# A new order from re-measured planner prices, one seven-product pair fewer, and a handicap for late GpSimd steps

## The chip, the cores and the metric

The kernel runs on one core of a Trainium2 chip. The metric is the device time of one execution in microseconds (us). TensorE (PE, its weight loads PEld) multiplies into PSUM, VectorE (DVE), ScalarE (ACT) and GpSimd (POOL) do the rest, and SyncE (SP) issues most DMA transfers. Each engine works through its own queue in order; steps on different engines are tied by semaphores.

## The reference

One pre-norm layer on x of 512 tokens x 1024 channels in float32, with two token mixers fed by one input projection:

```python
h = rmsnorm(x, norm_g)
(q_lat, c_kv, k_rope, z_a, q_b, k_b, v_b, z_b,
 q_idx, k_idx, w_idx, gate_a, gate_b) = jnp.split(h @ w_in, cuts, axis=-1)
# branch a: 8-head latent attention (low-rank q and kv, rotary key), causal in chunks of 64
y_a = mla_attention(q_nope, q_pe, k_nope, k_pe, v_a, pos) * silu(z_a)
# branch b: an indexer scores keys, each query keeps its top 128; relative bias; 8 heads
y_b = dsa_attention(q_b, k_b, v_b, q_idx, k_idx, w_idx, rel_bias, pos, topk) * silu(z_b)
merged = sigmoid(gate_a) * (y_a @ w_o_a) + sigmoid(gate_b) * (y_b @ w_o_b)
out = rmsnorm(x + merged @ w_out, final_g)
```

## The kernel before

**Products.** A number in float32 is split into a rounded high part and a rest (a cast on ScalarE, L370, and a subtraction on VectorE or GpSimd, L401 or L403), and each product is three matmuls (high x high, high x rest, rest x high; `mm3`, all recorded at L479). The input is held transposed and normalised as eight k-tiles `hT`. A projection tile of 128 output channels comes in one of two ways. `proj` (L1139), the plain one, multiplies eight k-tiles by all 512 tokens: 24 matmuls of 512 columns. `proj2` (L1203) takes two tiles as a 2 x 2 block product and needs seven products instead of eight (Strassen's scheme in Winograd's form): sums of weights and of inputs (`input_sums`, L1170, tiles `hs`) come first, each product is four k-tiles by 256 tokens, and `seven` (L1289) takes partial sums out of PSUM into the tiles `pair`.

**Stages.** The first 50 us load x and the first weights and make latents and indexer keys. Then come the projections of the a branch (gates `ga`, `za`, the MLA operands `ma`, values `va`) while the indexer's scores and the top-128 masks are made (`topk`, L964), with a's attention heads in between; then pairs of b's projections (`SB` keys and queries, `VB` values, `GB` gates, `ZB` the SiLU gates z_b) with b's heads in between. `branch_out` (L2076) multiplies each branch by its w_o, `merged` (L2050) splits the result, and `output` (L2279) multiplies by w_out, again by seven products numbered 1, 7, 2, 6, 5, 4, 3, whose weights are summed and split in `out_job` and `split_b` (L2134, L2125, tiles `wsum` and `wo`). `finish` and `scale_out` (L2187, L2227) add x, normalise and store. Gates of branch a are stored to HBM after their tanh (`gate`, L1462, transfer bias_scratch<-s_sig) and fetched back late.

**What sets the order.** The program is written as threads that yield steps; while it is built, a planner (`Flow`, L154, its loop `run` at L214) keeps a clock for each engine, prices every ready step, and emits the one that can start first. Steps with two possible engines (`BOTH`, VectorE or GpSimd) go where they would end first, with a handicap for GpSimd (`pbias`; `soon`, L393, sets it to 0, and `LATE` sets the general one once the last mask is made, L978). Prices stand in the step helpers: ScalarE in `act_opt` (L365), VectorE and GpSimd in `tt`, `ts` and `scale_by` (L397, L418, L426), TensorE in `stream` and `turn` (the transposes, L470 and L492). The delay of a semaphore is in `lat` (L156). A transfer's bytes over 360000 are its duration, times `SLOWER`, then `LAND` (L255 to L257). The chip's queues follow the order so planned; the prices themselves appear nowhere in the program that runs. `QUEUE` (L2446) is the list of projection and output jobs, with pairs in capitals. Further constants limit the slots a class may hold (`PHCAP`, `TCAP`, `PCAP`, `SPARE`) and set the priorities of threads.

## Time and profile before

| | |
|---|---|
| median of 3 runs | 425.13 us (423.97 to 425.34) |
| the profiled execution's own time | 425.56 us |
| its span, first to last instruction | 423.8 us, at a granted clock of 0.996 |
| ScalarE busy | 297.5 us (70%) |
| GpSimd busy | 100.9 us (24%) |
| DMA | 65.91 MB, mean 156 GB/s |

The span is the time between the first and the last instruction; the execution's own time is 1.8 us longer. A busy share is an average over all stages, and TensorE's busy time counts a matmul until its results are out, although the next one has begun by then. So the rows by stage and the waits say more than the shares.

### The profile page before, as it was taken

What the parts mean: (1) busy time and instruction counts of PE and PEld (TensorE: products, weight loads), DVE (VectorE), ACT (ScalarE), POOL (GpSimd) and SP (SyncE); (2) the same over time, 40 slices, a digit from 0 to 9 for tenths busy, and PEclk for the clock granted to TensorE, in tenths of its full rate; (3) what the DMA queues carried; (4) which work ended last, traced back from release to release, by engine and by line L of the source; (5) the groups of instructions that cost most, each with busy time, mean ns of one, the idle gap of its engine ahead of it and who ended that gap; (6) DMA issues with size and microseconds to landing.
All of it is one profiled execution on the core that took longest, in us unless ns stands there. A gap on an engine that the chain in (4) does not pass through costs nothing.

```text
span 423.8 us, 7541 instructions
## 1 busy us (share of the span) xinstructions
PE 413.6 (98%) x2487; PEld 368.8 (87%) x2487; DVE 378.7 (89%) x804; ACT 297.5 (70%) x682; POOL 100.9 (24%) x127
## 2 busy tenths in 40 slices
PE   9999999999999999999999999999999999999983
PEld 6999888898887888889999999999998888888863
DVE  4879789899999999997999789899869997999994
ACT  5796976479584967749786798997689744347534
POOL 1033764024344547541000012130001000010212
PEclk9999999999999999999999999999999999999998
DMA  8973345724644631442334737314633975566305
GB/s 266 394 285 101 116 137 183 182 57 110 202 104 152 179 111 49 125 113 76 113 130 105 200 95 199 95 65 136 187 113 125 336 254 200 182 201 209 134 1 199
DMA packets 30279, 65.91 MB, mean 156 GB/s; under 512 B 4648, under 2 KB 5688, under 8 KB 30240
## 3 DMA queue, kind: packets, MB, share of 16 engines
q1 hardware_dynamic: 29120, 63.82, 48.1%
q0 software_dynamic: 832, 1.22, 1.1%
q8 instruction: 19, 0.31, 0.3%
q10 hardware_dynamic: 288, 0.39, 0.3%
q14 instruction: 20, 0.16, 0.1%
HBM read 50.49 MB, written 4.21 MB: 129 GB/s over the span
## 4 chain that ended last, share of the span: by engine, by line
PE 65%; DVE 20%; ACT 5%; issue 4%; DMA 2%; POOL 1%; SPq 1%; POOLq 0%; DVEq 0%; ACTq 0%
PE ps L479 57%; PE ps L498 4%; DVE s_wo L401 2%; DVE s_mg L401 2%; ACT s_w L370 2%; DVE s_w L401 1%; DVE s_wsum L401 1%; DMA raw<-w_out 1%; DVE s_rg L401 1%; DVE s_x L413 1%; DVE mask L972 1%; DVE s_pair L401 1%; PE ps L606 1%; PE ps L946 1%; DVE s_xr L413 1%
## 5 line engine op out<-in xcount | busy, mean ns | idle before, releaser
L479 PE MATMUL ps<-s_h,s_w 128*128 128x512 f32 (+1 forms) x672 | 139.2, 350 | 0.0
L479 PEld LDWEIGHTS ps<-s_h,s_w 128*128 128x128 f32 x672 | 106.6, 189 | 13.4 <-ACT s_w L370 0.2
L370 ACT CAST s_w<-raw 128x512 fp32r<-128x512 f32 (+3 forms) x134 | 77.4, 596 | 18.5 <-DVE raw L401 9.3
L401 DVE TENSOR_TENSOR s_w<-raw,s_w 128x512 fp32r<-128x512 f32 (+2 forms) x104 | 67.1, 663 | 6.9 <-ACT s_w L370 6.2
L479 PE MATMUL ps<-s_hs,s_w 128*128 128x256 f32 x384 | 53.5, 285 | 0.0
L403 POOL TENSOR_TENSOR s_w<-raw,s_w 128x512 fp32r<-128x512 f32 (+2 forms) x30 | 35.0, 1173 | 77.6 <-DVE s_ys L413 36.9
L479 PEld LDWEIGHTS ps<-s_hs,s_w 128*128 128x128 f32 x384 | 49.2, 191 | 0.4
L479 PE MATMUL ps<-s_ys,s_w 128*128 128x512 f32 x192 | 43.7, 389 | 0.0
L479 PEld LDWEIGHTS ps<-s_ys,s_w 128*128 128x128 f32 x192 | 36.0, 188 | 7.6
L479 PE MATMUL ps<-s_wo,s_mg 128*128 128x512 f32 (+1 forms) x156 | 33.6, 374 | 1.2 <-ACT s_wo L370 0.9
L479 PEld LDWEIGHTS ps<-s_wo,s_mg 128*128 128x128 f32 x156 | 27.6, 188 | 7.0 <-ACT s_wo L370 1.3
L479 PE MATMUL ps<-s_w,s_xg 128*128 128x328 f32 (+1 forms) x192 | 32.9, 324 | 0.1
L479 PEld LDWEIGHTS ps<-s_w,s_xg 128*128 128x128 f32 x192 | 31.3, 188 | 0.6 <-ACT s_rbc L370 0.5
L379 ACT ACTIVATE s_p<-s_p,sm 128x512 f32<-128x512 f32 (+3 forms) x58 | 31.6, 564 | 0.1
L972 DVE MATCH_REPLACE8 mask<-sm,mask 128x256 f32<-128x256 f32 (+2 forms) x48 | 25.8, 540 | 0.0
L971 DVE MAX8 sm<-mask 128x8 f32<-128x256 f32 (+2 forms) x48 | 25.5, 547 | 0.3
L498 PE MATMUL ps<-ident,s_p 128*128 128x128 f32 x160 | 23.0, 274 | 0.0
L379 ACT ACTIVATE s_p<-ps,sm 128x128 f32<-128x128 f32 (+3 forms) x32 | 16.7, 525 | 8.9 <-DVE sm L1878 8.8
L370 ACT COPY s_tmp<-ps 64x512 f32<-64x512 f32 (+1 forms) x18 | 10.1, 562 | 15.5 <-PE ps L479 8.7
L498 PEld LDWEIGHTS ps<-ident,s_p 128*128 128x128 f32 x160 | 18.4, 140 | 2.6 <-DVE s_ph L401 0.5
L479 PE MATMUL ps<-s_lat,s_w 128*128 128x512 f32 x78 | 20.5, 394 | 0.0
L1977 DVE CUSTOM_DVE_ANT_0 s_p<-ps,mask 128x128 f32<-128x128 f32 (+3 forms) x32 | 15.3, 486 | 4.9 <-PE ps L479 4.7
(217 smaller groups left out, 798.4 us busy)
## 6 DMA issues: line engine op xcount, KB each, us to landing
raw<-w_out SPq DMA_DIRECT2D x18, 512.0 KB, 5.2
s_op<-s_op SPq DMA_DIRECT2D x36, 128.0 KB, 2.4
raw<-w_ga SPq DMA_DIRECT2D x8, 512.0 KB, 3.4
raw<-w_gb SPq DMA_DIRECT2D x8, 512.0 KB
raw<-w_o SPq DMA_DIRECT2D x16, 256.0 KB, 4.5
s_x<-xT SPq DMA_DIRECT2D x8, 256.0 KB, 4.0
s_xn<-x SPq DMA_DIRECT2D x8, 256.0 KB, 5.6
raw<-w_za SPq DMA_DIRECT2D x4, 512.0 KB, 5.0
```

Source lines behind the costliest of these rows:

```text
L370: nc.scalar.copy(dst.ap, src.ap)
L379: nc.scalar.activation(dst.ap, src.ap, func, **kw)
L401: opts.append(("DVE", 0.07 + 0.00104 * x.n, lambda: nc.vector.tensor_tensor(dst.ap, x.ap, y.ap, op=op)))
L403: opts.append(("POOL", 0.15 + 0.0021 * x.n, lambda: nc.gpsimd.tensor_tensor(dst.ap, x.ap, y.ap, op=op)))
L413: lambda: nc.vector.scalar_tensor_tensor(dst.ap, x.ap, sc(s), y.ap, op0=op0, op1=op1))],
L479: nc.tensor.matmul(ps.ap, l.ap, r.ap, start=start and i == 0, stop=stop and i == len(pairs) - 1, skip_group_check=more)
L498: nc.tensor.transpose(d.ap, s.ap, ident.tile)
L606: nc.tensor.matmul(ps.tile.rearrange("p (a b) -> p a b", b=P), z, z.rearrange("p (a b) -> p a b", a=1).to_broadcast([P, NT, P]), start=Tru ...
L946: yield pe(0.005 + n / 2400, [ps.all], [qs[h].all, ks[0].all], lambda: (product_to(ps[:, :n], True), nc.tensor.matmul(ps.tile[:, :n], qs[h ...
L971: yield Step([("DVE", t, lambda: nc.vector.max(m8.tile, work.ap))], [m8], [mask[i]])
L972: yield Step([("DVE", t + 0.068, lambda: nc.vector.match_replace(work.ap, m8.tile, work.ap, MARK))], [mask[i]], [m8])
L1977: step = Step([("DVE", 0.1 + 0.00104 * n, lambda: nc.vector.tensor_tensor_reduce(p.ap, ps.tile[:, :n], mask[i].tile, op0=ALU.add, op1=ALU. ...
```

## The change

Three things change, all of them in how the order is planned. First, the planner's prices: the delay before TensorE goes from 0.26 to 0.19 us, ScalarE's and VectorE's delays become a little shorter; steps on fewer than 128 partitions get 0.12 us more, some activations 0.075 to 0.1 more; a transpose goes from 0.109 to 0.0875, a 512-column matmul from 0.228 to 0.227; transfers after the first 25 us have three kinds (inside SBUF, loads, stores) with prices of their own. Second, the queue of jobs: ZB0 and ZB3 become plain tiles (zb0 right behind sb0, zb3 behind the last gate pair), and ZB1 and ZB2 form one pair. Third, the weight sums and rests of the output products other than 1, 7 and 2 carry a handicap of 0.4 us on GpSimd, and the general handicap after the last mask goes from 0.75 to 0.4. Limits of slots and priorities are set anew.

```diff
@@ Flow.lat
         if dst == "PE":
-            return 0.26
-        return {"PE": 0.2, "ACT": 0.15, "DVE": 0.16, "POOL": 0.08}[src]
+            return TO_PE
+        return {"PE": 0.2, "ACT": 0.14, "DVE": 0.12 if dst == "ACT" else 0.16, "POOL": 0.08}[src]
@@ Flow.run, a transfer of SP
-                self.hw = max(self.hw, s) + (0.65 if step.ins and step.outs else 0.475)
-                self.dma = max(self.dma, self.hw + 0.65) + dur * (SLOWER[bool(step.ins and step.outs)] if s > 25.0 else 1.0)
-                end = self.dma + (LAND if step.ins and step.outs else 1.5 if s < 0.77 or dur < 0.05 else 2.15 if s < 10.0 else 1.8 if s < 20.0 else 1.0) + step.late
+                kind = 0 if step.ins and step.outs else 1 if step.outs else 2
+                if s > 25.0:
+                    at = max(self.hw, s)
+                    self.hw = at + 0.59
+                    self.dma = max(self.dma, at + 1.0) + dur * SLOWER[kind]
+                    end = self.dma + LAND[kind] + step.late
...
@@ step helpers
+    def few(x):
+        return 0.12 if x.ap.shape[0] < P else 0
...
+    def late(step, product):
+        step.pbias = 0.0 if product in EARLY else LATE
+        return step
...
-        return max(0.0148 + n / 2400, 0.109) - 0.0015 * (n == 256)
+        return max(0.0134 + n / 2400, 0.109)
...
-        return pe(0.109 * len(parts), [d for d, _ in parts], [s for _, s in parts] + [ident.all], emit, len(parts))
+        return pe(0.0875 * len(parts), [d for d, _ in parts], [s for _, s in parts] + [ident.all], emit, len(parts))
...
-            yield Step([("DVE", t + 0.068, lambda: nc.vector.match_replace(work.ap, m8.tile, work.ap, MARK))], [mask[i]], [m8])
+            yield Step([("DVE", t - 0.009, lambda: nc.vector.match_replace(work.ap, m8.tile, work.ap, MARK))], [mask[i]], [m8])
@@ split_b and out_job
-        yield soon(lo_part(lo.all, raw, hi.all))
+        yield late(lo_part(lo.all, raw, hi.all), key[0])
...
-                    yield soon(tt(t, raw[i], t, ALU.add if product == 6 else ALU.subtract, BOTH))
+                    yield late(tt(t, raw[i], t, ALU.add if product == 6 else ALU.subtract, BOTH), product)
@@ constants
-PHCAP = 6
+PHCAP = 5
-TCAP = 6
-PTOPK = 15.0
-PSCORE = 12.0
+TCAP = 5
+PTOPK = 13.0
+PSCORE = 10.0
-QUEUE = 'ga0 ga1 pe ma0 ga2 za0 va1 va0 ma1 ga3 za1 ma2 ga4 ga5 ma3 za2 za3 sb0 ga6 ga7 VB SB1 GB0 GB1 SB2 ZB0 ZB1 GB2 GB3 SB3 GB4 GB5 ZB2 ZB3 gb6 ou ou gb7 ou'
-LATE = 0.75
+QUEUE = 'ga0 ga1 pe ma0 ga2 za0 va1 va0 ma1 ga3 za1 ma2 ga4 ga5 ma3 za2 za3 sb0 zb0 ga6 ga7 VB SB1 GB0 GB1 SB2 ZB1 ZB2 GB2 GB3 SB3 GB4 GB5 zb3 gb6 ou ou gb7 ou'
+LATE = 0.4
+EARLY = (1, 7, 2)
-YSB = 7
+YSB = 5
-LAND = 2.6
-SLOWER = 1.08, 2.0
+LAND = 1.5, 1.3, 1.4
+SLOWER = 1.8, 1.13, 1.09
+TO_PE = 0.19
-PLOW = 8.0
-PREST = 3.0
-SPARE = {'w': 2, 'wo': 6, 'sig': 3}
+PLOW = 9.0
+PREST = 8.0
+SPARE = {'w': 3, 'wo': 6, 'sig': 3}
-PSUMS = 5.0
-PCAP = 10
+PSUMS = 8.0
+PCAP = 11
-SUMS_AT = ('a', 5)
+SUMS_AT = ('a', 6)
```

More of the change, by code (lines that the diff above doesn't have):

```diff
@@ L254, in run @@
                 self.free["SP"] = s + 0.05
-                self.hw = max(self.hw, s) + (0.65 if step.ins and step.outs else 0.475)
-                self.dma = max(self.dma, self.hw + 0.65) + dur * (SLOWER[bool(step.ins and step.outs)] if s > 25.0 else 1.0)
-                end = self.dma + (LAND if step.ins and step.outs else 1.5 if s < 0.77 or dur < 0.05 else 2.15 if s < 10.0 else 1.8 if s < 20.0 else 1.0) + step.late
+                kind = 0 if step.ins and step.outs else 1 if step.outs else 2
[4 more added lines that the diff above has]
+                    end = self.dma + LAND[kind] + step.late
+                else:
+                    self.hw = max(self.hw, s) + (0.475 if kind else 0.65)
+                    self.dma = max(self.dma, self.hw + 0.65) + dur
+                    end = self.dma + (1.5 if s < 0.77 or dur < 0.05 else 2.15 if s < 10.0 else 1.8 if s < 20.0 else 1.0) + step.late
             else:
@@ L287 @@
 JITTER = 0
-SEED = 687
+SEED = 1
 DRAWN = random.Random(SEED)
@@ L363, in bufs @@
         return [v.buf for v in vs if isinstance(v, View)]
+    def few(x):
+        return 0.12 if x.ap.shape[0] < P else 0
     def act_opt(dst, src, func=AF.Copy, scale=None, bias=None, accum=None):
         t = (0.05 if in_ps(src) else 0.1) + 0.00083 * src.n + ((0.18 if in_ps(src) else 0.09) if accum is not None else 0) + (0.09 if isinstance(scale, View) else 0)
+        t += (0.1 if isinstance(bias, View) and not in_ps(src) else 0) + few(src) + (0.075 if func == AF.Square else 0)
         def emit():
@@ L400, in tt @@
             if e == "DVE":
-                opts.append(("DVE", 0.07 + 0.00104 * x.n, lambda: nc.vector.tensor_tensor(dst.ap, x.ap, y.ap, op=op)))
+                opts.append(("DVE", 0.07 + 0.00104 * x.n + few(x), lambda: nc.vector.tensor_tensor(dst.ap, x.ap, y.ap, op=op)))
             else:
@@ L418, in ts @@
     def ts(dst, x, s1, s2, op0, op1=None):
-        t = 0.1 + (0.00104 if in_ps(x) else 0.00052) * x.n
+        t = 0.1 + (0.00104 if in_ps(x) else 0.00052) * x.n + few(x) + 0.03 * isinstance(s1, View)
         kw = {} if op1 is None else {"op1": op1}
@@ L430, in scale_by @@
             if e == "DVE":
-                t = 0.1 + (0.00104 if in_ps(x) else 0.00052) * x.n
+                t = 0.13 + (0.00104 if in_ps(x) else 0.00052) * x.n
                 opts.append((e, t, lambda: nc.vector.tensor_scalar(dst.ap, x.ap, s.ap, None, ALU.mult)))
```

## The prediction, before the result was known

> **What bounds the kernel now.** I read the page first: the busy shares, then the slices.
>
> ```profile
> span 423.8 us, 7541 instructions
> PE 413.6 (98%) x2487; PEld 368.8 (87%) x2487; DVE 378.7 (89%) x804; ACT 297.5 (70%) x682; POOL 100.9 (24%) x127
> PEclk9999999999999999999999999999999999999998
> ```
>
> TensorE is busy 98% of the span at the full granted clock, and VectorE comes next with 89%. A time can therefore go down in three ways only: fewer or cheaper TensorE instructions, fewer waits of TensorE, or a shorter tail behind its last matmul. The 98% is not proof of no waits, because a matmul's busy time overlaps the next one's, so I read the busy time by stage next, and then who made TensorE wait. In the rows by stage the columns are the stretch, its length, and busy microseconds (instructions) of PE, PEld, DVE, ACT and POOL, then clock, DMA share and GB/s.
>
> ```profile
> 120.00:140.00 20.00, 19.38 (x106) 16.34 (x105) 19.03 (x51) 11.90 (x30) 9.13 (x12) 1.00 0.46 137
> 340.00:360.00 20.00, 20.00 (x90) 16.57 (x89) 16.12 (x28) 8.85 (x15) 0.00 (x0) 1.00 0.62 218
> 360.00:380.00 20.00, 20.00 (x90) 16.48 (x89) 19.97 (x38) 7.68 (x14) 1.93 (x3) 1.00 0.60 190
> 380.00:400.00 20.00, 20.00 (x93) 16.69 (x92) 19.29 (x37) 14.30 (x29) 1.59 (x2) 1.00 0.58 197
> 400.00:424.00 24.00, 15.89 (x88) 13.14 (x86) 18.47 (x39) 9.52 (x23) 4.82 (x6) 0.93 0.23 88
> ```
>
> From 340 to 400 us TensorE never stops, while VectorE is full (19.97 and 19.29 of 20). Only in the last 24 us does TensorE lose real time. The waits of TensorE, longest first, from the views of the weight loads and of the matmuls:
>
> ```profile
> PEld ps L479 <- ACT s_wo L370: 1.3, 1, 1.3
> PEld ps L1894 <- ACT s_p L379: 1.1, 1, 1.1
> PEld ps L498 <- DVE s_lat L413: 1.0, 1, 1.0
> PEld ps L479 <- DVE s_wo L401: 0.6, 1, 0.6
> PEld ps L479 <- ACT ps L370: 0.6, 3, 0.2
> PEld ps L498 <- DVE s_ph L401: 0.5, 2, 0.3
> PE ps L1894 <- ACT s_p L379: 0.6, 1, 0.6
> ```
>
> Apart from the start, these six groups are nearly the whole prize: 5.1 us of idling weight loads, of which the matmuls feel a part. No engine is to be relieved for its own sake.
>
> **Part one: one pair of ZB tiles becomes two plain tiles.** A pair by seven products is 7 x 4 k-tiles x 3 matmuls = 84 matmuls of 256 columns. Two plain tiles are 2 x 8 x 3 = 48 of 512 columns. Both rates stand in the timeline (start, us, count), in the first pair stage and the plain branch stage; two groups of the page follow, with busy time and mean ns of one:
>
> ```profile
> 209.90 3.04 PE L479 MATMUL ps<-s_w,s_h 128*128 128x256 f32 x24
> 212.78 3.04 PE L479 MATMUL ps<-s_w,s_hs 128*128 128x256 f32 x24
> 333.15 13.08 PE L479 MATMUL ps<-s_ys,s_w 128*128 128x512 f32 x57
> ```
>
> ```profile
> L479 PE MATMUL ps<-s_ys,s_w 128*128 128x512 f32 x192 | 43.7, 389 | 0.0
> L498 PE MATMUL ps<-ident,s_p 128*128 128x128 f32 x160 | 23.0, 274 | 0.0
> ```
>
> From 209.90 to 212.78 are 2.88 us for 24, so 0.120 us each. The 57 plain ones take 13.08 us with the last one's own duration (the 389 ns of the page's group) in it, so 12.69 / 56 = 0.227 each. The pair costs 84 x 0.120 = 10.08 us, the two tiles 48 x 0.227 = 10.90 us. **TensorE gets 0.82 us more work.** In a stage where it never rests this lands on the end in full.
>
> The Trainium skill ("TensorE: Matmul & The Clock Gate", section "Wait — 56ns, not 53.3ns?") gives a warm matmul its columns at 2.4 GHz plus about 2.5 ns; by that an estimate is 48 x 0.2158 - 84 x 0.1092 = 1.19 us more. The trace does not agree with the figure (0.227 and 0.120 measured), so the measured 0.82 stands.
>
> What the pair no longer asks of the other engines, from the groups kept apart by shape:
>
> ```profile
> L370 ACT CAST s_w<-raw 128x512 fp32r<-128x512 f32 x110 | 66.6, 621 | 17.6 <-DVE raw L401 9.3 <-DMA raw<-w_o 5.5 <-PE ps L479 2.0
> L401 DVE TENSOR_TENSOR s_w<-raw,s_w 128x512 fp32r<-128x512 f32 x89 | 59.7, 685 | 6.0 <-ACT s_w L370 5.3
> L370 ACT COPY s_pair<-ps 128x256 f32<-128x256 f32 x32 | 11.8, 369 | 7.8 <-PE ps L479 7.5
> L401 DVE TENSOR_TENSOR s_pair<-ps,s_pair 128x256 f32<-128x256 f32 x16 | 6.7, 419 | 1.1 <-PE ps L479 0.8 <-ACT s_pair L370 0.3
> ```
>
> Seven splits become four, four sums of weights go, and five copies and two adds out of PSUM go. On ScalarE that is 3 x 0.62 + 5 x 0.37 = 3.7 us, on VectorE and GpSimd together (3 + 4) x 0.69 + 2 x 0.42 = 5.7 us. None of it is on TensorE's path by itself. It can help only by removing the small waits (ACT ps 0.6, DVE s_ph 0.5) of the attention heads that share this stage. I bound that between 0 and -1.1 and take -0.5, near the middle, since the rows name those engines but each wait is under 0.3. The input sums are also free one pair earlier, and the gated branch can be split sooner; nothing in TensorE's rows waits for these, so 0.
>
> **Part two: the planner's prices.** They emit no instruction; they change which step comes next on each engine. Only their fit to the trace can be judged before:
>
> ```profile
> s_op<-s_op SPq DMA_DIRECT2D x36, 128.0 KB, 2.4
> bias_scratch<-s_sig SPq DMA_DIRECT2D x8, 256.0 KB, 3.8
> 151.38 0.79 PE ps L498 x7
> L370 ACT COPY s_tmp<-ps 64x512 f32<-64x512 f32 x16 | 9.3, 582 | 14.9 <-PE ps L479 8.7 <-DMA bias_scratch<-s_sig 5.9
> L370 ACT COPY s_pair<-ps 128x512 f32<-128x512 f32 x4 | 2.3, 582 | 0.0
> ```
>
> A 128 KB move inside SBUF was priced 0.65 + 0.65 + 0.364 x 2.0 + 2.6 = 4.63 us and becomes 1.0 + 0.364 x 1.8 + 1.5 = 3.16; it lands in 2.4. A 256 KB store was 0.475 + 0.65 + 0.728 x 1.08 + 1.0 = 2.91 and becomes 1.0 + 0.728 x 1.09 + 1.4 = 3.19; it lands in 3.8. Both come closer. Two prices move away: a transpose goes from 0.109 to 0.0875 where seven take 0.79 (0.113 each), and a step on fewer than 128 partitions gets 0.12 more on its engine, where 64 and 128 partitions both take 582 ns. So the plan is better on transfers and not better all over.
>
> The transfers matter at one place. At 135 us ScalarE has waited long for the slot of a stored gate, and TensorE pays soon after:
>
> ```profile
> 135.21 0.58 ACT L370 COPY s_tmp<-ps 64x512 f32<-64x512 f32 x1 [5.87 <-DMA bias_scratch<-s_sig]
> 137.85 0.45 PE L1894 MATMUL ps<-s_op,qhi 100*128 100x384 f32 x1 [0.62 <-ACT s_p L379]
> ```
>
> The idle 0.62 and the 0.16 us by which a 512-column matmul outlasts the next one's start (0.389 less 0.227) make 0.8 us. With a longer price for the store and a shorter one for the moves, this copy should no longer sit first in ScalarE's queue: **-0.8 us** (bounds 0 and -1.8; the second takes in the wait for s_lat, 1.0 at the weight load, which I leave standing). The moved zb0 (ahead of ga6), the tighter limits on slots and the new priorities have no row of their own; I give them 0, with the bounds of the sum of all these waits on one side and of the second and third rival on the other.
>
> **Part three: fewer late GpSimd steps.** In the output stage the sums and rests of products 6, 5, 4 and 3 get a handicap of 0.4 us on GpSimd where they had none; other steps that two engines can do have theirs lowered from 0.75 to 0.4 once the last mask is made, so GpSimd may take more in the attention stages, at no price for TensorE while VectorE is not ahead of it. What it did there, and what came behind the last one:
>
> ```profile
> 393.68 1.30 POOL L403 TENSOR_TENSOR s_wo<-s_wsum,s_wo 128x512 fp32r<-128x512 f32 x1 [13.39 <-ACT s_wo L370]
> 400.08 1.30 POOL L403 TENSOR_TENSOR s_wo<-s_wsum,s_wo 128x512 fp32r<-128x512 f32 x1 [5.10 <-DVE s_wo L401]
> 401.05 1.48 DVE L401 TENSOR_TENSOR s_part<-s_part,s_part 128x512 f32<-128x512 f32 x2
> 396.65 1.28 DVE L401 TENSOR_TENSOR s_wsum<-raw,s_wsum 128x512 f32<-128x512 f32 x2
> 406.22 1.29 POOL L403 TENSOR_TENSOR s_wsum<-raw,s_wsum 128x512 f32<-128x512 f32 x1 [4.84 <-DVE s_xr L401]
> 408.55 0.60 ACT L370 CAST s_wo<-s_wsum 128x512 fp32r<-128x512 f32 x1
> 405.67 2.65 PE L479 MATMUL ps<-s_wo,s_mg 128*128 128x512 f32 x11
> 409.20 0.51 PE L479 MATMUL ps<-s_wo,s_mg 128*128 128x512 f32 x1 [0.88 <-ACT s_wo L370]
> 409.99 1.43 PE L479 MATMUL ps<-s_wo,s_mg 128*128 128x512 f32 x5 [0.28 <-DVE s_wo L401]
> ```
>
> GpSimd makes a sum of weights until 407.51, its cast on ScalarE ends at 409.15, and TensorE resumes at 409.20. The run before ended at 408.32 with a matmul whose next could have started 0.16 us earlier, so 409.20 - 408.16 = 1.04 us are lost; the next start, 409.99, is 0.79 after instead of 0.23, so 0.56 more. **1.6 us**, the largest single loss. On VectorE the sum (half of 1.28 for two, 0.64) would be done by 406.9 from the same start. I take -1.6, with bounds 0 and -1.6. The price of moving three steps is 3 x 0.64 = 1.9 us on a full VectorE if TensorE's stock of operands runs out, and 0 while it holds, as it did from 340 to 408. I take 0. The moved steps issue no DMA and pass no queue of SP.
>
> The two VectorE sums at 401.05 took 1.48 beside a GpSimd step, against 1.28 alone: 0.20 us lost per such meeting, so three moved steps also give VectorE back up to 0.6. The Trainium skill ("SBUF — State Buffer", section "SBUF: two separate sides") has the port pair that the two share as an exclusive lock for a whole instruction; the trace agrees in direction, with 0.20 of a 1.30 us step.
>
> **Sum.** +0.82 - 0.5 - 0.8 - 1.6 + 0 = -2.1 us. The profiled execution took 425.56 us (span 423.8 and 1.76 around it), 0.43 above the median 425.13 of the runs; 425.56 - 2.1 = 423.5 there, 425.13 - 2.1 = **423.0** for the median. The tail behind the last matmul stays as it is.
>
> **The rivals.**
> *The waits only move.* TensorE's order is new in all stages, and VectorE, full from 360 to 400, leaves its last operands as late as before. For it: the 1.6 us came after 40 us of a full VectorE, and its total in that stage hardly falls. Against it: GpSimd and ScalarE, not VectorE, made the last sum late. Then +0.82 stays, only the -0.8 counts, and the time is about 425.1, no difference. A measurement of this kernel can tell about 0.3%, 1.3 us.
> *The late steps overfill VectorE, and it is slower.* If TensorE's stock runs out before 400, each step that GpSimd would have taken costs TensorE 0.64 us: 425.13 + 0.82 + 1.9, with the old 1.6 still there, is 427.9. It decides from the point where VectorE has no idle time ahead of the last rests, and 19.97 of 20 is near. Against it: the pair's 5.7 us of steps are gone from the stage ahead.
> *The plan with too cheap transposes is no better.* The heads' 160 transposes are now planned 0.0215 us shorter, 3.4 us in all, so plan and chip part by more; data is then early rather than late at TensorE, but buffers come free late. If two waits as large as the one at 137.85 return in the attention stages: 425.13 + 0.82 + 2 x 0.8 - 1.6 = 426.0, within what can be told from no change.
>
> **How the numbers follow.** The forecast has 0.57; waits that move and the plan that is no better together 0.25; the overfull VectorE 0.18. The likeliest case reaches from all bounds down (425.13 + 0.82 - 1.1 - 1.8 - 1.6 = 421.4, and 0.6 less with VectorE's gain, 420.9) up to 423.8. Both unchanged cases lie between 425 and 426.1. Of the slower case the lower half, to 426.6, is inside. So 420.9 to 426.6. Faster 0.57, same 0.25, slower 0.18.
>
> **What would show it.** In the changed profile: 28 copies s_pair<-ps of 256 columns instead of 32 (four a pair, so seven pairs), 2451 TensorE instructions; the line "ACT s_wo" gone from TensorE's waits, and no 512-column GpSimd step after about 390; the store of a gate no longer ahead of a 5.87 us wait of ScalarE. I am wrong if TensorE's waits sum to as much as before at other places, or if it stops for VectorE's s_wo rests between 380 and 410.

## The result and the profile after

The changed kernel takes 427.75 us in the median of five executions (426.87 to 429.5), the kernel before 425.13 (423.97 to 425.59). The ratio is 1.0073, 95% interval [1.0056, 1.0091]: slower by about 2.6 us. The forecast was 423.0 in a range from 420.9 to 426.6, so the time went the other way and lies outside the range. The profiled execution of the changed kernel is the slowest of its five, 429.5 us with a span of 427.7. That matters below.

The page of the changed kernel, its first lines and the slices of the granted clock:

```profile
span 427.7 us, 7455 instructions
PE 415.5 (97%) x2451; PEld 369.4 (86%) x2451; DVE 375.5 (88%) x801; ACT 293.5 (69%) x669; POOL 101.6 (24%) x126
PEclk9999999989999999999999999999999999999998
```

TensorE has the 36 matmuls less that the pair's end was to bring, VectorE and ScalarE have 3.2 and 4.0 us less to do, and there is one slice more with a lower clock, the ninth, which begins near 85 us. By stage, with the columns as in the prediction; the first line is the kernel before, the others the changed one:

```profile
80.00:100.00 20.00, 20.00 (x127) 18.10 (x126) 19.59 (x53) 13.33 (x34) 3.46 (x8) 1.00 0.37 107
80.00:100.00 20.00, 18.16 (x107) 16.57 (x106) 16.06 (x47) 11.10 (x31) 3.52 (x6) 0.91 0.15 46
120.00:140.00 20.00, 20.00 (x110) 17.16 (x109) 19.67 (x47) 13.55 (x34) 9.24 (x13) 1.00 0.55 158
240.00:260.00 20.00, 19.35 (x154) 18.77 (x154) 15.43 (x42) 15.92 (x44) 0.00 (x0) 1.00 0.51 151
300.00:320.00 20.00, 19.48 (x138) 17.86 (x138) 17.86 (x34) 15.20 (x37) 0.00 (x0) 1.00 0.74 228
400.00:424.00 24.00, 20.38 (x113) 17.55 (x111) 22.18 (x45) 11.97 (x28) 4.83 (x6) 0.99 0.17 61
```

The stage from 120 to 140 us is better than before (20.00 against 19.38), the one from 80 to 100 is worse (18.16 against 20.00, and 20 matmuls fewer in it). The waits of TensorE's weight loads in the changed kernel name the new ones:

```profile
PEld ps L1910 <- DMA s_op<-kpel: 2.0, 1, 2.0
PEld ps L494 <- ACT s_pair L381: 1.5, 3, 0.8
PEld ps L494 <- ACT s_w L381: 1.0, 2, 0.6
PEld ps L1909 <- ACT s_p L390: 0.8, 2, 0.5
PEld ps L513 <- POOL rstd L468: 0.6, 1, 0.6
```

The waits that the prediction meant to remove are out of this list: the one for s_wo near 409 us, and the one for s_p at 137.85 (the 0.8 for s_p lies at other places). The small ones of the heads that it named (ACT ps, DVE s_ph) are gone too. Others stand instead. From the starts of all matmuls in the two traces I took what each interval has above the pace of its shape (0.227 us for 512 columns, 0.120 for 256). The stream without that excess is 400.1 us before and 400.9 after; the excess is 15.7 before and 18.2 after. So the last matmul starts 3.3 us later (416.77 and 420.10), and the tail behind it is 0.6 us longer (7.0 and 7.6 to the end of the span): the 3.9 us between the spans. By stage the excess grew by 3.4 us from 80 to 100 us, by 1.5 from 240 to 320 and by 1.0 in the first 40; it shrank by 0.8 from 40 to 60, by 0.9 from 120 to 140 and by 1.7 behind 400.

**The wait at 85 us.** TensorE of the changed kernel, then the queue of SP, each with start and duration, then how long the move took from issue to landing:

```profile
79.48 2.91 PE L494 MATMUL ps<-s_h,s_w 128*128 128x512 f32 x12
82.23 0.87 PE L494 MATMUL ps<-s_w,s_lat 128*128 128x256 f32 x6
82.94 0.22 PE L1909 MATMUL ps<-s_op,qhi 100*128 100x128 f32 x1
85.00 0.33 PE L1910 MATMUL ps<-s_op,qhi 96*128 96x128 f32 x1 [1.84 <-DMA s_op<-kpel]
```

```profile
76.93 0.85 SPq L523 DMA_DIRECT2D s_op<-kpeh  x1
77.89 0.40 SPq L523 DMA_DIRECT2D raw<-w_ga  x1
78.35 0.42 SPq L523 DMA_DIRECT2D bias_scratch<-s_sig  x1
78.82 0.58 SPq L523 DMA_DIRECT2D s_op<-kpel  x1
```

```profile
s_op<-kpel SPq DMA_DIRECT2D x2, 64.0 KB, 6.1
```

The first logits of an a head start at 82.94, and their second matmul needs the 64 KB move of kpel. The move is issued behind a 512 KB load of w_ga and a 256 KB store of a gate on the same queue and lands 6.1 us after its issue. The kernel before issues the move behind the same load and store, but 27 value matmuls go first on TensorE from 82.36 us on, so that its logits come at 85.58 and find the data there:

```profile
82.36 3.38 PE L479 MATMUL ps<-s_w,s_lat 128*128 128x256 f32 x27
85.58 0.22 PE L1894 MATMUL ps<-s_op,qhi 100*128 100x128 f32 x1
```
The planner's price of such a move by itself fell from 0.65 + 0.65 + 0.182 x 2.0 + 2.6 = 4.26 to 1.0 + 0.182 x 1.8 + 1.5 = 2.83 us, both far under 6.1, and the plan now puts the logits ahead. Every order below that the planner made with the new price of the moves has this wait in some size, and none made with the old price has it.

**The end.** GpSimd of the changed kernel behind 396 us, and its TensorE:

```profile
398.67 1.29 POOL L418 TENSOR_TENSOR s_wsum<-raw,s_wsum 128x512 f32<-128x512 f32 x1 [25.85 <-DVE s_wsum L416]
403.65 1.30 POOL L418 TENSOR_TENSOR s_wo<-s_wsum,s_wo 128x512 fp32r<-128x512 f32 x1 [3.69 <-DVE s_wsum L416]
414.79 1.31 POOL L418 TENSOR_TENSOR s_wo<-raw,s_wo 128x512 fp32r<-128x512 f32 x1 [9.84 <-DVE s_wo L416]
```

```profile
397.83 16.92 PE L494 MATMUL ps<-s_wo,s_mg 128*128 128x512 f32 x85
414.58 5.80 PE L494 MATMUL ps<-s_wo,qhi 128*128 128x512 f32 x36
```

There are still three GpSimd steps of 512 columns behind 390 us, as many as before, but TensorE runs through to its last matmul. The 1.6 us of waits are gone, and the time is not shorter.

### The profile page after: what moved, and what is told of

The parts are those of the page before. It is cut to its first block, busy times and chain, and to the rows that moved or that the text cites. A ratio compares the mean times of both kernels' runs of the same rounds, so it can differ in the third digit from the quotient of the medians.

```text
span 427.7 us, 7455 instructions
## 1 busy us (share of the span) xinstructions
PE 415.5 (97%) x2451; PEld 369.4 (86%) x2451; DVE 375.5 (88%) x801; ACT 293.5 (69%) x669; POOL 101.6 (24%) x126
## 4 chain that ended last, share of the span: by engine, by line
PE 63%; DVE 17%; DMA 9%; ACT 5%; issue 3%; SPq 2%; POOL 0%; POOLq 0%; ACTq 0%; DVEq 0%
PE ps L494 54%; PE ps L513 5%; DVE s_w L416 2%; DVE s_wo L416 2%; DMA raw<-w_o 2%; DVE s_mg L416 2%; ACT s_w L381 2%; SPq L523 2%; DMA s_op<-kpel 1%; DMA raw<-w_ql 1%; DMA s_x<-xT 1%; DMA s_xn<-x 1%; DVE s_pair L416 1%; DVE s_rg L416 1%; PE ps L1910 1%
## 5 line engine op out<-in xcount | busy, mean ns | idle before, releaser
L494 PE MATMUL ps<-s_h,s_w 128*128 128x512 f32 (+1 forms) x684 | 149.5, 357 | 1.1 <-ACT s_pair L381 0.6
L494 PEld LDWEIGHTS ps<-s_h,s_w 128*128 128x128 f32 x684 | 110.3, 189 | 15.6 <-ACT s_pair L381 1.5
L381 ACT CAST s_w<-raw 128x512 fp32r<-128x512 f32 (+3 forms) x132 | 76.0, 595 | 22.0 <-DMA raw<-w_o 12.7
L416 DVE TENSOR_TENSOR s_w<-raw,s_w 128x512 fp32r<-128x512 f32 (+2 forms) x95 | 62.1, 674 | 3.9 <-ACT s_w L381 3.5
L418 POOL TENSOR_TENSOR s_w<-raw,s_w 128x512 fp32r<-128x512 f32 (+2 forms) x37 | 44.5, 1207 | 61.7 <-ACT s_w L381 30.7
L494 PE MATMUL ps<-s_hs,s_w 128*128 128x256 f32 x336 | 46.7, 285 | 0.0
L494 PEld LDWEIGHTS ps<-s_hs,s_w 128*128 128x128 f32 x336 | 42.8, 191 | 0.4 <-DVE s_w L416 0.2
L390 ACT ACTIVATE s_p<-s_p,sm 128x512 f32<-128x512 f32 (+3 forms) x52 | 28.7, 571 | 0.1
L494 PE MATMUL ps<-s_lat,s_w 128*128 128x512 f32 x78 | 20.7, 397 | 0.0
```

The costliest lines, as they stand in the source:

```text
L381: nc.scalar.copy(dst.ap, src.ap)
L390: nc.scalar.activation(dst.ap, src.ap, func, **kw)
L416: opts.append(("DVE", 0.07 + 0.00104 * x.n + few(x), lambda: nc.vector.tensor_tensor(dst.ap, x.ap, y.ap, op=op)))
L418: opts.append(("POOL", 0.15 + 0.0021 * x.n, lambda: nc.gpsimd.tensor_tensor(dst.ap, x.ap, y.ap, op=op)))
L494: nc.tensor.matmul(ps.ap, l.ap, r.ap, start=start and i == 0, stop=stop and i == len(pairs) - 1, skip_group_check=more)
```

## The experiments

The times of each group of runs stand beside the kernel before on the same chip; ratios are to that. "Replayed" means that the planner follows a recorded list of (thread, engine), so that only the entries named differ in the program; "planned anew" means that the planner chose again, and that every stage may differ.

### What the wait at 85 us costs

Replayed order of the changed kernel, with three moves put forward (the first kpeh is ahead of the load already):

```diff
 SP queue near 77 us
 s_op<-kpeh
+s_op<-kpel, s_op<-kpeh, s_op<-kpel
 raw<-w_ga
 bias_scratch<-s_sig
-s_op<-kpel, s_op<-kpeh, s_op<-kpel
```

> The changed kernel in its own order, with four steps of SyncE's queue moved and nothing else: the four key moves (s_op<-kpeh, s_op<-kpel) are issued ahead of the 512 KB load of w_ga and the 256 KB store of a gate that they followed. Theory A (TensorE's 2.0 us wait at 85 us comes from moves that land in order behind that load and store): the moves land by about 81 us, the wait and the stretch at half clock behind it go, and the median falls by the 2.0 us of the wait, 427.75 to about 425.8, or by up to 3.6 where an execution also had the half clock. Rival B (the changed order loses in many small places, and a wait that is removed returns at the next full buffer or late operand): under 0.7 us of it arrives at the end, 427.1 to 427.8.

426.63 us (425.67 to 427.05) against 424.65, ratio 1.0046 [1.0033, 1.0059]. TensorE in this run, where the second matmul follows the first at once:

```profile
83.11 0.22 PE L2106 MATMUL ps<-s_op,qhi 100*128 100x128 f32 x1
83.18 0.28 PE L2107 MATMUL ps<-s_op,qhi 96*128 96x128 f32 x1
```

Set beside the profiled execution of the changed kernel, TensorE is 3.2 us ahead at 91 us and still 3.2 us ahead at its last matmul: nothing of it is given back. In the medians it is much less, from 1.0073 to 1.0046, with intervals that overlap a little. So the profiled execution overstates the wait: its mean granted clock is 0.991, that of the four other executions 0.993 to 0.994, and the run without the handicap (below) shows a shorter wait at the same place.

Of the 3.2 us the wait itself is 1.9. The rest is in the clock: behind the wait the granted clock was 0.5 from 85.6 to 89.0 us. To keep it up without touching the wait, nine matmuls of zeros went into the bank that the head is about to use; their product is overwritten and read by nothing.

```diff
+for _ in range(9): matmul(bank, zero, zero)   # ahead of the first head's logits
```

> The changed kernel in its own order, with nine matmuls on zeros (0.216 us each) into the PSUM bank of the first attention head, just ahead of its logits, so that TensorE computes instead of waiting at 83 to 85 us; the moves land as late as before. Theory A with the clock (the wait costs twice, because the granted clock falls to one half for 3.4 us behind it in the profile): the wait stays 2 us long but the clock stays full, the profiled execution falls by about 1.7 us (429.5 to 427.8); the median falls by 1.7 too if all executions had the half clock, by little if only the profiled one had. Rival (the half clock is only shown and costs nothing, or comes from something else): the median stays at 427.75 within 0.4.

428.98 us (428.49 to 429.4), 1.0106 [1.0092, 1.0119]. The clock stayed at 1.0 there, and TensorE gained 1.6 us on the changed kernel's profile between 85 and 92 us. But the median rose. The nine matmuls themselves hold TensorE from 83.89 to 85.66 us, also in an execution where the move would have been only a little late; and in the profiled execution the weight load behind GpSimd's power for rstd waited 1.9 us at the start instead of 0.6. Which of the two raised the median is not shown. The clock's part is seen in the profile; as a price in the median this run is inconclusive.

Old prices of the moves alone, planned anew:

```diff
-LAND = 1.5, 1.3, 1.4
-SLOWER = 1.8, 1.13, 1.09
+LAND = 2.9, 1.3, 1.4
+SLOWER = 2.0, 1.13, 1.09
```

> The changed kernel with the planner's price of moves inside SBUF as long as before (LAND 2.9 and SLOWER 2.0 for them), all else as changed; the order from 70 us on is planned anew. Theory A (the shorter price is what put the first logits ahead of their keys): the 2.0 us wait at 85 is gone from TensorE's waits, median about 425.8. Rival B (any new plan loses as much in other places): no wait at 85, but others, and a median between 426.5 and 430.

430.35 us (429.43 to 431.43), 1.0147 [1.013, 1.0164]. The wait at 85 us is gone, as it should be, and the time is worse. Its list begins with a wait that in the changed kernel is 0.6 in all:

```profile
PEld ps L494 <- DVE s_w L416: 3.0, 3, 2.4
```

### Parts of the change, planned anew

The new prices and limits with the old list of two ZB pairs, the first part of the change alone, and the change without it:

```diff
 e4  QUEUE of before, all else changed
 e8  before, with lat(), the transfer prices and the step prices of the change
 e10 the change, with the price table of before
```

> The changed kernel with the queue of jobs of before (ZB0 ZB1 and ZB2 ZB3 as two pairs), all else as changed: the order is the same up to about 170 us, so the wait at 85 us stays. Theory C (the plain ZB tiles cost what they add to TensorE, 0.8 us, and little else): the median falls by 0.8 to about 426.9. Rival (the queue is the main cause, by what the plain tiles displace at 240 to 320 us): it falls by 2 or more, to 425.7 or below. Rival B (a new plan loses elsewhere): it rises above 427.75.

432.12 us (431.58 to 434.9), 1.0196 [1.0169, 1.0223]; the wait for kpel is there with 2.0 us, and many others behind 195 us.

> The first part of the change alone: all prices of the changed kernel, with the queue of jobs, limits, priorities and handicaps of before. Theory A (the better transfer prices are sound but for the moves): the wait at 85 us costs 2 us, the rest gains as much, 1.000 to 1.004. Rival B (queue, limits and prices were chosen together, and any order planned with one of them replaced loses 3 us or more to waits all over, as the two re-planned kernels did with 1.0147 and 1.0196): 1.007 or more, with waits at several places between 190 and 320 us.

430.97 us (428.53 to 432.66), 1.0142 [1.0115, 1.017]; kpel 2.8 us in two waits, s_pair 3.4 in four.

> The change without its first part: the new list of pairs, the handicap for late GpSimd steps and the new limits and priorities, but the price table of before; planned anew. Theory A (the scatter of orders, not a price, decides; the table was only right together with the rest): slower than the changed kernel, 428 to 434 us, with no wait of TensorE behind a kpeh or kpel move near 85 us, but others. Rival B (the new price of the moves is the whole loss, and what the other parts bring is intact): 423 to 425.5 us, no wait over 1 us between 40 and 400 us.

429.87 us (429.65 to 430.12), 1.0113 [1.01, 1.0127]. No wait for kpel, but 2.9 us in four for s_pair. The rival, that the move's price was the whole loss, has nothing for it here; what rules it out is the run with the moves forward, which has no such wait and still stands at 1.0046 [1.0033, 1.0059].

Each of these variants is worse than the whole change. Before reading that as the parts needing one another, the plain question is what a new plan costs that changes nothing. The planner adds a small constant times a thread's priority (20 at most) to each candidate's start. A change of the constant by 0.001 shifts one candidate against another by less than 0.03 us, so it decides near ties alone; the constant stands for nothing on the chip.

```diff
-BIAS = 0.01
+BIAS = 0.011   # e9 on before, e16 on the changed kernel; e15 on before with 0.009
```

> The kernel before with a single planner constant changed that stands for nothing on the chip: the weight of a thread's number in the comparison of candidates, 0.010 to 0.011. It computes the same, with the same instructions on TensorE, but 623 of the 1,106 TensorE steps of the plan stand elsewhere. Theory A (each re-planning gives an order whose small waits are drawn anew, and the order of before is a lucky one of many): slower than before by 0.5 to 2%, 427 to 433 us, with two to five new TensorE waits of 0.5 to 2.5 us that before does not have. Rival B (the plan's order is worth the same unless prices or products change; the losses of the variants came from their parts): within 0.3% of before, 424 to 426.5 us.

426.31 us (425.18 to 426.67), 1.0026 [1.0014, 1.0038].

> The kernel before with the weight of a thread's number in the planner's comparison at 0.009 instead of 0.010: a second neutral order, with 744 of 1,106 TensorE steps elsewhere. Theory A (scatter: an order drawn anew is worth a few tenths to 2% less than the chosen one): 426 to 432 us. Rival B (neutral orders agree within 0.3% and the parts tried alone lost for reasons of their own): 424 to 426.5 us.

429.06 us (428.48 to 429.92), 1.0106 [1.0087, 1.0124].

> The changed kernel with the same constant at 0.011: a neutral order of the changed plan, with 519 of 1,066 TensorE steps elsewhere, the first at step 302. Theory A (the changed order is itself a chosen one, so most others are worse): 428 to 434 us. Rival B (the changed kernel's loss is an unlucky draw): 424 to 426.5 us, at or below the kernel before.

430.88 us (430.1 to 431.55), 1.0149 [1.0128, 1.017].

The longest new wait of each of these three, in that order:

```profile
PEld ps L479 <- ACT s_pair L370: 1.6, 2, 1.3
```

```profile
PEld ps L479 <- ACT s_ys L379: 2.6, 1, 2.6
```

```profile
PEld ps L1910 <- DMA s_op<-kpel: 2.0, 2, 1.8
```

Three orders that differ by such ties alone cost 0.26%, 1.06%, and (1.0149 beside 1.0073) some 0.75%. The four variants above lie between 1.1 and 2.0%, so most of what they lost is of the size of this scatter, and they say nothing sure about prices, queue or limits. All three redrawn orders are slower than the order they were drawn from, as they would be if both kernels were picked orders; three draws don't show more, and how the two were found is not on record. The change's +0.73% is itself within the scatter. My theory of 0.5 to 2% was too high for the first of the three, which by itself fits the rival, that neutral orders agree within 0.3%; the second and the third rule that rival out.

### The start

In the changed kernel GpSimd's power for rstd stands in the plan behind a VectorE step of another thread, since the planner keeps the two engines off their shared port: it starts at 27.41 us. Replayed with the moves forward as above, and with that one rule left out for GpSimd's powers, of which this 4-column step is the first:

```diff
+        step.alone = True
-                    elif step.fenced and self.pair:
+                    elif step.fenced and self.pair and not step.alone:
```

> The changed kernel with the key moves ahead of load and store (as in the first experiment), and GpSimd's small powers no longer ordered behind a VectorE step by the planner's rule for the port that the two share; the queues are otherwise the same. In the changed kernel the power for rstd waited 24.74 us until VectorE's s_w of 27.3 us; without that order it can start at 23.5 us. Theory A (the loss is a few named waits, and each comes off in full): TensorE's wait for rstd (0.5 to 0.8 us) and the one for s_rbc behind it (0.3) go, so the time falls by 0.8 to 1.1 us below the first experiment's 1.0046 of before, to 1.002 to 1.003. Rival B (the start is bound by the loads, and TensorE waits there for something else): 1.004 to 1.005.

426.02 us (425.64 to 426.26) against 424.18, 1.0036 [1.0024, 1.0048]. The power starts at 24.00 and the wait of 0.6 is gone; beside the 1.0046 without it the intervals overlap, so the median can't tell the 0.4 us. The two edits together are worth some 0.37% of the 0.73%. What leads this run's list then is the attention of the b branch:

```profile
PEld ps L694 <- ACT s_pair L579: 1.8, 3, 0.8
PEld ps L694 <- ACT s_w L579: 0.9, 2, 0.6
```

### The handicap

```diff
-        step.pbias = 0.0 if product in EARLY else LATE
+        step.pbias = 0.0
```

> The change without its third part: the handicap on the late GpSimd steps is nought for every product, all else as in the changed kernel, planned anew. The plan then differs from the changed kernel's in one GpSimd step, seven VectorE places and two ScalarE places, all in the last 25 us, and in no TensorE place. Theory A (the handicap moved next to nothing and is worth nothing): within 0.3% of the changed kernel, 426.5 to 429 us. Rival B (the handicap is what took the tail's waits away): 0.8 to 1.6 us slower than the changed kernel, with waits of TensorE back near 408 to 412 us.

427.38 us (426.66 to 428.19) against 424.81, 1.006 [1.0046, 1.0073]: the changed kernel within its scatter. So the handicap of the output products did nothing by itself; the plan is the same but for one GpSimd step and a few places at the end. The other half of the third part, the general handicap of 0.4 instead of 0.75, stands in this run too and was not tried by itself. Since TensorE's order is the same as in the changed kernel, this run also shows another execution of the place at 85 us:

```profile
83.14 0.22 PE L1909 MATMUL ps<-s_op,qhi 100*128 100x128 f32 x1
83.50 0.33 PE L1910 MATMUL ps<-s_op,qhi 96*128 96x128 f32 x1
```

Here the move was 0.25 us late, not 1.9, and the clock stayed at 1.0. The span is 424.9, not 427.7. The loss at 85 us differs from one execution to the next: 0.2 us here, 3.4 with the half clock in the other profile.

### Why TensorE's waits near 409 us were worth nothing

All five runs are the kernel before, replayed. First the late sum alone went to VectorE, at its place:

```diff
-POOL s_wsum<-raw,s_wsum   at 406.2
+DVE  s_wsum<-raw,s_wsum   at the same place of the plan
```

> The kernel before with one step on another engine: the weight sum of product 4 that GpSimd made at 406.2 us is made by VectorE at the same place of the order. The prediction's theory (GpSimd's 1.29 us is what made the cast and TensorE late): TensorE's 1.6 us of waits at 408 to 410 shrink by 0.6 to 1.6 us, ratio to before 0.9965 to 0.9985. Rival (the cast stands behind three squares in ScalarE's queue, which end at 408.65 whoever makes the sum, and VectorE, now with 0.6 us more, lets the squares start later): no gain, or 0.3 to 0.6 us slower, 1.000 to 1.0015.

425.25 us (424.17 to 427.42) against 424.18, 1.0026 [1.0012, 1.0041]. TensorE's weight loads waited 1.4 and 1.1 us for s_wo. The sum was done at 406.95 us, but ScalarE took up its cast only at 407.83, behind three squares; in the kernel before the cast likewise starts at 408.55, right behind the squares and 1.04 us after GpSimd's sum. (The profiled execution of this run also had the clock at 0.5 from 410.2 to 413.6 us, so its end is not compared.) So the sum went ahead of the evictions, its cast ahead of ScalarE's squares, and its rest ahead of the three multiplications by the gain:

```diff
 DVE
+s_wsum<-raw,s_wsum
 s_xr<-ps,s_xr x3
+s_wo<-s_wsum,s_wo
 s_rg<-s_xr,s_fg x3
 ACT
+s_wo<-s_wsum
 junk<-s_xr (squares)
```

> The kernel before with that sum on VectorE and ahead of the evictions of 406.07 us, the cast of the sum ahead of the squares in ScalarE's queue, and the rest (s_wo) ahead of the final gains in VectorE's. Theory (the queue order at ScalarE and VectorE, not GpSimd's speed, made TensorE wait): the operands are there by 408, the two waits (1.6 us) go and the end comes 1.0 to 1.6 us earlier, 0.996 to 0.998. Rival (VectorE is full, what is put ahead pushes product 3's rests back, and TensorE waits for those): no change, 0.9985 to 1.001.

424.98 us (424.11 to 425.45), 1.0014 [1.0005, 1.0023]. TensorE and VectorE of this run, then VectorE and TensorE in the trace of before:

```profile
401.73 7.52 PE L677 MATMUL ps<-s_wo,s_mg 128*128 128x256 f32 x37
409.09 5.80 PE L677 MATMUL ps<-s_wo,qhi 128*128 128x512 f32 x36
```

```profile
407.44 1.35 DVE L599 TENSOR_TENSOR s_rg<-s_xr,s_fg 128x512 f32<-128x512 f32 x3
408.71 1.88 DVE L599 TENSOR_TENSOR s_wo<-raw,s_wo 128x512 fp32r<-128x512 f32 x3
410.52 1.28 DVE L611 SCALAR_TENSOR_TENSOR s_xr<-ps,s_xr 128x512 f32<-128x512 f32 x2
```

```profile
402.46 3.69 DVE L401 TENSOR_TENSOR s_xr<-s_xr,s_part 128x512 f32<-128x512 f32 x6
411.07 1.27 DVE L413 SCALAR_TENSOR_TENSOR s_xr<-ps,s_xr 128x512 f32<-128x512 f32 x2
411.26 5.79 PE L479 MATMUL ps<-s_wo,qhi 128*128 128x512 f32 x36
```

TensorE doesn't stop: its last 36 matmuls start at 409.09, in the trace of before at 411.26. The end is not earlier by that: the last matmul starts 2.2 us earlier (414.61 against 416.77), and the span is 0.6 shorter. VectorE has no pause here from 401 to 414 us. It runs 1.1 us earlier than in the trace of before at the six sums ahead of these lines (401.36 against 402.46), but only 0.55 earlier at the evictions of product 4 (410.52 against 411.07), since it has the late sum to do as well. That VectorE's backlog sets the end was then tried by taking the three multiplications off it, first to GpSimd:

```diff
-DVE  s_rg<-s_xr,s_fg x3 (512, 256, 256 columns)
+POOL s_rg<-s_xr,s_fg x3
```

> The run in which the late sum and the cast stood first, with one thing more: the three multiplications by the gain for products 1 and 2 of the output (one of 512 columns, two of 256) are on GpSimd and not on VectorE, so that VectorE has 1.27 us less to do ahead of product 3's rests; all other steps keep their places. Theory A (VectorE's backlog, not TensorE's waits, sets the end from 400 us on): 0.5 to 1.3 us faster than that run, 423.7 to 424.5 us by the median, with the rests of product 3 begun 0.8 to 1.3 us earlier against the last value matmul and the evictions of product 4 as much earlier. Rival B (something else behind the last matmul, the scaling and the stores, sets the end): within 0.3 us of that run, the tail behind the last matmul longer by what the rests gained. Rival C (GpSimd's multiplications come too late for the scaling that reads them): slower by 0.5 us or more, with ScalarE or VectorE waiting for GpSimd near 405 us.

425.24 us (424.71 to 425.96) against 424.81, 1.0013 [1.0003, 1.0023]: no gain. GpSimd and VectorE of this run show where it went:

```profile
407.99 4.07 POOL L601 TENSOR_TENSOR s_rg<-s_xr,s_fg 128x512 f32<-128x512 f32 x3 [7.37 <-DVE s_wo L599]
```

```profile
407.77 2.99 DVE L599 TENSOR_TENSOR s_wo<-raw,s_wo 128x512 fp32r<-128x512 f32 x3
410.68 1.28 DVE L611 SCALAR_TENSOR_TENSOR s_xr<-ps,s_xr 128x512 f32<-128x512 f32 x2
```

VectorE starts the three rests earlier, but they take 2.99 us beside GpSimd and not 1.88, and the evictions behind them start at 410.68, where they were at 410.52. Of the 1.27 us taken off VectorE, 1.11 came back in these three steps. So the same three multiplications were left out, once in the order of before and once with the sum and cast first; the output lacks the gain in half of its columns for two of the four token tiles.

```diff
-yield soon(tt(y, r, fg[half], MULT))
+if half == 0 or t < 2:
+    yield soon(tt(y, r, fg[half], MULT))
```

> The kernel before in its own order, with the multiplications by the gain for the second half of the last two tiles of tokens left out (three VectorE instructions, 1.27 us, ahead of product 3's rests; the output lacks the gain there, and the scaling reads the sums themselves). TensorE's two waits near 409 us are not touched: they stand behind ScalarE's cast and VectorE's first rest. Theory A (VectorE's backlog sets the end): the three later rests begin 1.2 us earlier against the first rest, and the time falls by 0.6 to 1.3 us, to 423.5 to 424.2 us. Rival B (TensorE's waits set the end): TensorE reaches product 3 no earlier than before, the rests end while TensorE is still on product 4, and the time stays within 0.3 us of before.

424.3 us (423.68 to 425.29) against 424.46, ratio 1.0 [0.9988, 1.0011].

> The run in which the late sum and the cast stood first, with the same three multiplications left out (the output lacks the gain there). Both of TensorE's waits near 409 us are gone and VectorE has 1.27 us less ahead of product 3's rests, without any GpSimd step beside them. Theory A (VectorE's backlog sets the end once TensorE is out of the way): 1.0 to 1.4 us faster than that run, 423.4 to 424.0 us, with the rests of product 3 at 1.88 us for three. Rival B (what follows the last matmul sets the end whatever VectorE did before): within 0.3 us of that run, 424.7 to 425.3 us.

423.57 us (422.9 to 424.72), 0.9983 [0.9972, 0.9995].

The last place of VectorE's rests in the first of the two, and in the second:

```profile
407.81 0.69 DVE L599 TENSOR_TENSOR s_wo<-s_wsum,s_wo 128x512 fp32r<-128x512 f32 x1 [1.12 <-ACT s_wo L568]
```

```profile
406.66 0.68 DVE L599 TENSOR_TENSOR s_wo<-s_wsum,s_wo 128x512 fp32r<-128x512 f32 x1
407.26 1.96 DVE L599 TENSOR_TENSOR s_wo<-raw,s_wo 128x512 fp32r<-128x512 f32 x3
409.13 1.28 DVE L611 SCALAR_TENSOR_TENSOR s_xr<-ps,s_xr 128x512 f32<-128x512 f32 x2
```

From the start of the six sums to the end of the span these traces say the same as the medians: 21.3 us before, 21.8 with the sum first, 21.3 without the multiplications, 20.7 with both.

Sum and cast moved alone bring no gain. VectorE's work removed alone brings none, since VectorE then waits 1.12 us for the same cast. Both together bring 0.31% against the run with the sum first (1.0014 to 0.9983, the intervals apart), about 1.3 us where 1.27 were left out; against the kernel before it is 0.17%. So two paths, the late sum with its cast behind ScalarE's squares and VectorE's own queue, reach the last rests at nearly the same time, and each covers the other. The first expectation of the theory fell (I had thought VectorE alone sets the end), its second held. No run with the full computation beats the kernel before.

## Why the prediction was wrong, by its own steps

**+0.82 for the pair: right.** The matmuls fell by the 36 that the working had (84 less 48), and the stream without its waits grew from 400.1 to 400.9 us.

**-0.5 for the small waits of the heads: failed.** The step took them as relieved by work that ScalarE and VectorE no longer have. The work did go (28 copies s_pair<-ps of 256 columns instead of 32), and the two groups of waits that the step named left the list, but TensorE's excess from 240 to 320 us grew by 1.5 us, in new waits for s_pair and s_w of 0.8 us at most. Fewer steps on an engine did not make its results earlier where TensorE needs them; which step of the order delays them was not tried.

**-0.8 at 137.85 us: gone in the rows, but no gain to count.** ScalarE's 5.87 us wait for the store is gone:

```profile
L381 ACT COPY s_tmp<-ps 64x512 f32<-64x512 f32 x16 | 9.3, 582 | 11.1 <-PE ps L494 10.9
```

The idle time ahead of this copy is TensorE's now, with no store in it. But in the runs that replay the order of before, TensorE's excess at that place is under 0.12 us in two and 0.3 to 0.45 in three, with nothing changed there. The 0.8 was that execution's, not the kernel's.

**-1.6 at the end: the step that decides.** It took the 1.6 us until "TensorE resumes at 409.20" and behind it for time lost to the end. The waits left the trace as forecast, but no time came back for them. In the order of before, where steps could be moved alone, the run with the sum first has none of them and is no faster (1.0014), and the time fell (0.9983) only when VectorE had less to do as well. In the changed kernel TensorE's excess behind 400 us is 1.7 us smaller, while the tail behind its last matmul is 0.6 longer. A view that the prediction didn't read had it: the chain that ended last. In the kernel before it leaves TensorE here (start, length, what) and is, but for one transfer and short pieces of ScalarE, GpSimd and issue, VectorE's from then to the end (a cut is marked by dots):

```profile
327.22 19.48 PE ps L479 x88
346.70 0.04 issue
...
357.67 1.20 DVE s_wo L401 x2
```

From 347 us on TensorE has no piece of that chain; in the changed kernel it leaves TensorE at 352. "Only in the last 24 us does TensorE lose real time" was true of TensorE, and not of the kernel.

**The blame on GpSimd and its handicap: wrong.** GpSimd's sum ended at 407.51, and what held the cast until 408.55 were ScalarE's squares; with the sum on VectorE the waits stayed. The handicap moves one step, and without it the time is the same. The mark "no 512-column GpSimd step after about 390" failed: there are three.

**0 for the prices, the list's order and the limits: mis-sized, and the sign with it.** This is where the part of the loss that the runs show came from. The price of a 128 KB move was called closer because it lands in 2.4 us by the median; the one that mattered has 64 KB, stood behind 0.75 MB on its queue and took 6.1. It cost from 0.2 to 3.4 us by execution, and 0.6 to 1.1 us in the medians (1.006 and 1.0073 with this order, 1.0046 with the moves ahead). The start cost 0.6 by its row. With both put right the ratio is 1.0036, so half of the +0.73% is left; it is within the 0.3 to 1.1% that three redrawn orders cost here, for which the prediction had no term, and which waits make it up in the median stays open.

**The rivals.** The one on the slower side gave 427.9, next to the measured 427.75, but by another mechanism: the old 1.6 us did not stay, and TensorE lost nothing between 340 and 400 us, where that rival had its price. "The waits only move" was right in kind: the excess rose by 2.5 us and did not fall, where that rival let the 0.8 count. That is also the prediction's own sign of being wrong, waits that sum to as much as before at other places. Whether the transposes' cheaper price makes the waits in the heads was not tried by itself and stays open; so does which limit or priority moved which step.

## What to carry to other kernels

Read the chain that ended last before you count a wait as a gain: a wait of the busiest engine is worth nothing while another engine's queue reaches the end at the same time, and both have to be shortened together. When a change has a planner draw a new order, measure first what a meaningless redraw costs; here it was 0.3 to 1.1%, or 1.1 to 4.5 us, where the whole forecast gain was 2.1 us, and parts tried alone in a new order showed little else. A term that rests on one wait in one execution needs a second execution before it is counted.

## What the runs showed of the hardware

A move of 64 KB landed 6.1 us after its issue behind a load of 512 KB and a store of 256 KB on the same queue, and with the same order on TensorE and on that queue the matmul behind it was 0.25 us late in one execution and 1.9 in another. After the 1.9 us wait the granted clock fell to 0.5 for 3.4 us. In the run with two ZB pairs the same wait of 1.9 us left the clock at 1.0, so the length of the wait alone doesn't decide it. With the late sum on VectorE, two TensorE waits of 0.98 and 0.83 us close together were followed by the clock at 0.5 for 3.4 us as well, from 410.2 us on. The Trainium skill ("TensorE: Matmul & The Clock Gate", section "Part 1: The HAM clock gate (the "warmup" mystery)") has a free-running window of about 3.4 us and a slow clock after one idle window; the trace agrees with the length of the slow stretch, and equal waits with unequal ends fit a window whose place counts, but here a wait of little over half a window was enough.

Three VectorE steps of 512 columns with both inputs in SBUF took 2.99 us beside GpSimd's three multiplications and 1.88 without: 1.11 us lost. The Trainium skill ("SBUF — State Buffer", section "SBUF: two separate sides") has the port pair that the two share as an exclusive lock for a whole instruction. Here the trace agrees better, though not in full, than the prediction had it: one after another the six steps would take 1.88 us, 1.30 for GpSimd's 512 columns and twice 0.74 for its 256 (a step of that size on the page of the changed kernel), 4.66 in all, and together they ran from 407.77 to 412.06, 4.29 us. The prediction's 0.20 per meeting came from a GpSimd step that ended 0.33 us after the VectorE steps began (401.38 and 401.05), so it was most of that overlap, not a small part of 1.30.
